# Values of two attention tiles as one group, and transposes moved between logits and scores, in an fp32 encoder layer

## The chip, the cores and the metric

The kernel runs on one core of one Trainium2 chip. The metric is the device time of one execution in microseconds. One more execution is recorded by the hardware profiler; the times of engines and instructions come from that one.

## The reference, cut to what matters

One encoder layer is applied to a prompt of 256 tokens and to a sample of 1024 tokens, all fp32, with a model width of 1024. After a normalisation and one wide projection, two attention branches run beside each other. Branch A has 8 heads of 64 with 2 key/value heads, a window of 128 to either side, a learned bias and a sink; branch B is a dilated mixture with 12 heads. Sigmoid gates merge both, then come an output projection and a squared-ReLU MLP. Branch A for one sequence is:

```python
s = einsum('bnqgrd,bnkgd->bngrqk', qb, kb) * (dh ** -0.5)
logits = where(valid, s + bias, NEG_INF)
m = maximum(max(logits, axis=-1), sink)
p = exp(logits - m[..., None])
denom = sum(p, axis=-1) + exp(sink - m)
o = einsum('bngrqk,bnkgd->bnqgrd', p, vb) / denom
...
merged = gates[:, :, 0] * (o_a @ w_branch_a) + gates[:, :, 1] * (o_b @ w_branch_b)
```

## The kernel before, in words

Tokens are cut into 10 tiles of 128 rows (8 of the sample, 2 of the prompt). The eight heads of branch A are four units of two heads. `order` lists the 40 pairs of unit and tile, and a loop takes two tiles per step: `for j in range(0, n + 2, 2)` with `n = 40`.

For one tile `scores` (lines 1063 to 1079) multiplies queries by the keys of the tile and its neighbours, two multiplications per head into one of two PSUM banks called `sc` (lines 1071, 1072). W is 384 keys, or 256 at the ends of a sequence. VectorE adds the bias and finds the row maximum in one instruction (line 1073), and writes the negated maximum (line 1077). `exponential` (line 1083) is one ScalarE instruction per head. `transposes` (line 1095) turns the probabilities block by block on TensorE: up to four blocks go into one bank `pt`, which ScalarE copies out (line 271), the remaining two into a second one, which VectorE copies out (line 273). There are two `pt` banks. `values_of` (line 1108) multiplies values by the turned probabilities. Its two heads fill the two halves of the partitions of one bank `pv`, of which there is one; the profile shows the form of these multiplications as 128\*64, where the others are 128\*128. VectorE copies the 128x128 result to a buffer `o` (line 1111, three buffers), and GpSimd's queue stores it to `scr_o[t]` (line 1112).

The same loop takes in other work, which its steps hand out piece by piece:

- `fill = logits()` multiplies the last gate columns of the wide projection. One `next(fill)` issues four 128x512 multiplications or eight 128x256 ones (line 192), three times per step. When a block of columns and tokens ends, the next `next(fill)` first issues ScalarE's copy of the result (line 1133) and its store, and after the 256-token block also `prepare()`: ScalarE rounds the next raw weights (line 231) and VectorE subtracts (line 235).
- `merges` combines the groups of branch B, four pieces per merge (lines 1165 to 1186), two pieces per step. The first piece also issues the loads of the next merge's rows on GpSimd's queue (lines 1146 to 1157) and ends in a small exponential on ScalarE (line 1169).
- `turn_merged` and `low_b` turn the merged rows of branch B in the last two full steps (lines 1214, 1222, 1226).

Each engine executes its own instructions in the order in which the program writes them here: `last.enter_context(tc.manual_schedule(engines=ALL))` fixes this until `last.close()`, after the loop and a short tail of it. What follows, the branch projections with `load_o` (line 1232), `turn_a` (lines 1250 to 1257), `low_a` (line 1261), the gates, and the rest of the layer, is ordered by a planner from its own estimates. `load_o(t)` loads the stored values of all units of a tile back, and `turn_a(t)` divides them by the sums of the exponentials, which `widen` (line 1240) spreads on GpSimd.

Of the kernel before, what the change touches and what calls it, by code (L numbers as in the profile page):

```python
# [15 lines left out]
P = 128  # L16
# [81 lines left out]
def encoder_kernel(  # L98
# [178 lines left out]
    scr_b = [dram.tile([T, 2, ROW], F32, name=f"scr_b{g}_") for g in range(3)]  # L277
    scr_o = [dram.tile([P, AH * HD], F32, name=f"scr_o{t}") for t in range(NT)]
    scr_x = [dram.tile([P, D], F32, name=f"scr_x{t}") for t in range(NT)]
# [769 lines left out]
    if True:  # L1049
# [13 lines left out]
        def scores(u, t):  # L1063
            st, bias = units[u]
            lo, W, c0 = tiles[t]
            s = a3("s", n=4)
            m = small.tile([P, 2], F32, name="m", tag="m")
# [31 lines left out]
        def values_of(u, t):  # L1099
            lo, W, _ = tiles[t]  # L1100
            pt = live.pop((u, t))
            v, rest = units[u][0]["v"]
            pv = bank("pv")
            for b in range(W // P):
                k = lo + b
                src = v[:, k, HALVES[u // 2]] if k < 8 else rest[:, k - 8, HALVES[u // 2]]
                for h in range(2):
                    nc.tensor.matmul(pv[HALVES[h], :P], src, pt[:, 2 * b + h, :],  # L1108
                                     start=b == 0, stop=b == W // P - 1, skip_group_check=True)
            o = a3("o", (P, P), 3)  # L1110
            nc.vector.tensor_copy(o, pv[:, :P])
            nc.gpsimd.dma_start(scr_o[t][:, P * u : P * u + P], o)

# [87 lines left out]
    if True:  # L1201
# [28 lines left out]
        def load_o(t):  # L1230
            rows_o[t] = slot("o", (P, 4, P))
            nc.sync.dma_start(rows_o[t], scr_o[t].rearrange("p (u q) -> p u q", u=4))

# [8 lines left out]
        def turn_a(t):  # L1242
            if t in (0, 4, 8):
                o_hi.block(t // 4)
                o_lo.block(t // 4)
            o = rows_o.pop(t)
            ps = bank("pt")
# [24 lines left out]
        for j in range(0, n + 2, 2):  # L1272
            if j < n:
                scores(*order[j])
                next(fill)
                if j > 2:
                    next(merges, None)
                next(fill)
                for h in range(2):
                    exponential(*order[j], h)  # L1280
                scores(*order[j + 1])
                next(fill)
                if j >= n - 4:
                    turn_merged(j - n + 4, "mm")
            if j:
                transposes(*order[j - 2])
            if j < n:
                exponential(*order[j + 1], 0)
            if j > 2:
                values_of(*order[j - 3])  # L1290
            if j:
                transposes(*order[j - 1])
            if j < n:
                exponential(*order[j + 1], 1)
            if j >= n - 4 and j < n:
                low_b(j - n + 4)
                turn_merged(j - n + 5, "mm")
            if j:
                values_of(*order[j - 2])
                if j > 2:  # L1300
                    next(merges, None)
            if j >= n - 4 and j < n:
                low_b(j - n + 5)
            if j < n and order[j][1] == 0 and order[j][0] < 3:
                u = order[j][0] + 1
                units[u] = load_unit(u), load_bias(u, lambda name, shape: a3(name, shape, 2))
            if j in (n - 6, n - 4):
                fetch()
            if j == n - 2:
                load_o(0)  # L1310
                load_o(1)
        next(fill)
        prepare()
        next(fill)
        values_of(*order[n - 1])
        run(merges)
# [570 lines left out]
```

## Time and profile before

| what | us |
|---|---|
| median of 3 runs (1727.32 to 1727.78) | 1727.51 |
| the profiled execution's own time | 1728.73 |
| its span, first to last instruction | 1727.0 |
| TensorE busy (matmuls, 98% of the span) | 1696.0 |
| TensorE weight loads busy (83%) | 1432.4 |
| VectorE / ScalarE / GpSimd busy | 978.5 / 727.4 / 525.7 |
| the loop of branch A, from about 562 to 712 | 150 |

PE stands for TensorE's matmuls and PEld for its weight loads, which overlap the matmuls; DVE is VectorE, ACT is ScalarE, POOL is GpSimd and SP the queue that issues most DMAs. A row of the timeline gives the start, the duration, the engine, the line, the operation, what is written and read with the shape, how many such instructions were put together, and in brackets the idle time of the engine ahead of it with what ended it. A row of the groups gives count, busy time, the mean duration in ns, and the idle time ahead of the group by what ended it. In a table of stretches there follow, after the bounds and the length, the busy times of PE, PEld, DVE, ACT and POOL, the granted clock, and the share and rate of DMA.

### The profile page before, as it was taken

The numbers are of one execution on the slowest core, as the hardware profiler recorded it, in microseconds if no ns is written. First come the engines' busy times: TensorE is split into PE (matmuls) and PEld (weight loads), VectorE is DVE, ScalarE is ACT, GpSimd is POOL, SyncE is SP. The second block draws the span as 40 slices with busy tenths as digits, with TensorE's granted clock in tenths as the row PEclk, the third lists the DMA queues.
The fourth block names the chain that finished last, engine by engine and source line by source line (L and its number), as shares of the span: only waits on it lengthen the run. The fifth ranks groups of instructions, "written<-read, shape, count | busy, mean of one in ns | idle before, by whom it ended". The sixth has DMA issues, their size and how long they took to land.

```text
span 1727.0 us, 25208 instructions
## 1 busy us (share of the span) xinstructions
PE 1696.0 (98%) x9248; PEld 1432.4 (83%) x9248; DVE 978.5 (57%) x1708; ACT 727.4 (42%) x1528; POOL 525.7 (30%) x462
## 2 busy tenths in 40 slices
PE   7999999999999999999999999999999999999998
PEld 6898888888888888788888788888888888888886
DVE  6733323445553577677458554545456786667575
ACT  6232223355553555655166433333334333333344
POOL 0212222212222354300100455555565442304050
PEclk9999999999999999999999999999999999999999
DMA  6414343576566753556012344334436834633333
GB/s 238 145 43 139 116 136 95 150 196 179 168 173 177 218 165 102 187 200 241 25 73 74 109 133 156 130 118 142 156 124 243 301 130 163 209 117 116 116 116 122
DMA packets 214779, 256.35 MB, mean 148 GB/s; under 512 B 24887, under 2 KB 144523, under 8 KB 214528
## 3 DMA queue, kind: packets, MB, share of 16 engines
q1 hardware_dynamic: 201424, 228.26, 41.0%
q0 software_dynamic: 12144, 24.38, 4.6%
q10 hardware_dynamic: 1088, 2.10, 0.3%
q8 instruction: 73, 1.20, 0.3%
q14 instruction: 50, 0.41, 0.1%
HBM read 169.10 MB, written 90.73 MB: 150 GB/s over the span
## 4 chain that ended last, share of the span: by engine, by line
PE 85%; DVE 4%; issue 3%; ACT 2%; DMA 2%; POOL 2%; SPq 0%; ACTq 0%; POOLq 0%; DVEq 0%
PE dn L351 21%; PE x L351 18%; PE mm L192 11%; PE z L351 9%; PE v L739 6%; PE pv L351 5%; PE mm L351 5%; PE y L351 4%; PE pv L566 2%; PE sc L522 1%; PE pt L553 1%; PE tr L342 1%; PE pv L1108 1%; PE pt L1095 1%; DVE clo L318 1%
## 5 line engine op out<-in xcount | busy, mean ns | idle before, releaser
L351 PE MATMUL dn<-dhi,ulo 128*128 128x512 f32 x448 | 174.7, 390 | 3.0 <-DVE ulo L186 3.0
L351 PE MATMUL dn<-dhi,uhi 128*128 128x512 f32 x448 | 174.3, 389 | 0.0
L351 PE MATMUL dn<-dlo,uhi 128*128 128x512 f32 x448 | 174.3, 389 | 0.0
L351 PE MATMUL x<-chi,wlo 128*128 128x512 f32 x424 | 167.6, 395 | 2.1 <-DVE u L1760 1.4
L351 PE MATMUL x<-clo,whi 128*128 128x512 f32 x424 | 165.7, 391 | 0.1
L351 PE MATMUL x<-chi,whi 128*128 128x512 f32 x424 | 165.1, 389 | 0.0
L318 DVE TENSOR_TENSOR wlo<-ta,whi 128x1024 fp32r<-128x1024 f32 x30 | 55.8, 1858 | 180.4 <-ACT whi L316 180.4
L318 DVE TENSOR_TENSOR wlo<-raw,whi 128x1024 fp32r<-128x1024 f32 x60 | 93.7, 1561 | 101.8 <-ACT whi L316 101.8
L393 POOL TENSOR_TENSOR tb<-raw 128x512 f32<-128x512 f32 x25 | 32.6, 1303 | 335.8 <-PE mm L192 113.5
L351 PEld LDWEIGHTS dn<-dhi,ulo 128*128 128x128 f32 x448 | 84.1, 188 | 21.7 <-DVE ulo L186 4.2
L186 DVE TENSOR_TENSOR ulo<-uraw,uhi 128x1024 fp32r<-128x1024 f32 x56 | 93.1, 1682 | 11.7 <-ACT uhi L185 11.7
L351 PEld LDWEIGHTS dn<-dhi,uhi 128*128 128x128 f32 x448 | 84.1, 188 | 17.6
L351 PEld LDWEIGHTS dn<-dlo,uhi 128*128 128x128 f32 x448 | 84.1, 188 | 17.2
L351 PEld LDWEIGHTS x<-chi,wlo 128*128 128x128 f32 x424 | 79.7, 188 | 20.3 <-issue 3.1
L351 PEld LDWEIGHTS x<-chi,whi 128*128 128x128 f32 x424 | 79.6, 188 | 17.1
L351 PEld LDWEIGHTS x<-clo,whi 128*128 128x128 f32 x424 | 79.8, 188 | 14.8 <-DVE clo L318 0.4
L1585 POOL TENSOR_TENSOR t<-raw,t 128x1024 f32<-128x1024 f32 x16 | 47.1, 2958 | 142.0 <-DMA raw<-in_w_down_dram 142.0
L1736 DVE TENSOR_TENSOR v<-v,dn 128x512 f32<-128x512 f32 x90 | 59.6, 683 | 42.8 <-PE dn L351 37.7
L1832 POOL TENSOR_TENSOR u<-u,u 128x640 f32<-128x640 f32 x16 | 25.6, 1597 | 165.1 <-ACT u L1757 165.1
L351 PE MATMUL pv<-phi,wlo 128*128 128x256 f32 x256 | 72.5, 283 | 1.7 <-ACT u L1756 1.7
L351 PE MATMUL dn<-dhi,up 128*128 128x512 f32 x224 | 73.5, 389 | 0.0
L543 ACT ACTIVATE s<-s,o 128x128 f32<-128x128 f32 (+1 forms) x120 | 51.9, 434 | 50.6 <-DVE o L535 46.6
(338 smaller groups left out, 4737.4 us busy)
## 6 DMA issues: line engine op xcount, KB each, us to landing
scr_u<-u SPq DMA_DIRECT2D x112, 320.0 KB, 2.6
uraw<-scr_u SPq DMA_DIRECT2D x56, 512.0 KB, 4.3
raw<-in_w_in_dram SPq DMA_DIRECT2D x33, 512.0 KB, 5.9
raw<-in_w_up_dram SPq DMA_DIRECT2D x32, 512.0 KB, 5.3
raw<-in_w_down_dram SPq DMA_DIRECT2D x28, 512.0 KB, 6.7
sg<-scr_g SPq DMA_DIRECT2D x32, 256.0 KB, 4.9
uraw<-scr_u SPq DMA_DIRECT2D x28, 256.0 KB, 4.4
v<-scr_v SPq DMA_DIRECT2D x96, 64.0 KB, 2.4
```

The lines of the kernel that those rows point to most:

```text
L186: nc.vector.tensor_tensor(lo, src, hi.bitcast(F32), op=ALU.subtract)
L192: nc.tensor.matmul(ps, a, b, start=i == 0, stop=i == len(seq) - 1)
L318: nc.vector.tensor_tensor(lo, src, hi.bitcast(F32), op=ALU.subtract)
L342: nc.tensor.transpose(ps[:, P * i : P * (i + 1)], xn[t][:, P * k : P * (k + 1)], ident)
L351: nc.tensor.matmul(ps, a, b, start=first and i == 0, stop=last and i == len(seq) - 1, skip_group_check=True)
L393: (nc.vector if vector else nc.gpsimd).tensor_tensor(o, x, y, op=ALU.subtract)
L543: nc.scalar.activation(s[:, h, :W], s[:, h, :W], AF.Exp, bias=nm[:, h : h + 1], accum_out=l[:, h : h + 1])
L566: nc.tensor.matmul(pv[p0 : p0 + nq, HD * h : HD * h + HD], pt[:, 2 * k + h, p0 : p0 + nq], v[:, a + k, HALVES[h]], start=k == 0, stop=k == ...
L739: nc.tensor.matmul(ps[:, :n], a, b, start=k == 0 and j == 0, stop=k == KC - 1 and j == 2)
L1585: nc.gpsimd.tensor_tensor(o, a, b, op=ALU.subtract)
L1736: nc.vector.tensor_tensor(v, v, ps, op=ALU.add)
L1832: nc.gpsimd.tensor_tensor(u[S1], u21, u22, op=ALU.add)
```

## The change

Four things change.

- `values_of(u, t)` now handles tiles t and t + 1. Their results stand beside each other in one `pv` bank, and one VectorE copy of 128x256 and one store move both. `o` has two buffers of 128x2x128.
- A step's values come one step later, all together between the step's first and second piece of `fill`. The transposes of the earlier step's first tile stand behind that second piece and ahead of the second tile's `scores`, and those of its second tile behind the third piece, at the step's end.
- The exponentials of the step's second tile stand behind both transposes. The first merge piece stands behind the values. The score buffer `s` has three buffers in place of four.
- `scr_o` holds pairs of tiles. `load_o` loads a pair at once, and `turn_a` takes its half.

```diff
-    scr_o = [dram.tile([P, AH * HD], F32, name=f"scr_o{t}") for t in range(NT)]
+    scr_o = [dram.tile([P, 4, 2, P], F32, name=f"scr_o{t}") for t in range(0, NT, 2)]
...
-            s = a3("s", n=4)
+            s = a3("s", n=3)
...
         def values_of(u, t):
-            lo, W, _ = tiles[t]
-            pt = live.pop((u, t))
-            v, rest = units[u][0]["v"]
+
             pv = bank("pv")
-            for b in range(W // P):
-                k = lo + b
-                src = v[:, k, HALVES[u // 2]] if k < 8 else rest[:, k - 8, HALVES[u // 2]]
-                for h in range(2):
-                    nc.tensor.matmul(pv[HALVES[h], :P], src, pt[:, 2 * b + h, :],
-                                     start=b == 0, stop=b == W // P - 1, skip_group_check=True)
-            o = a3("o", (P, P), 3)
-            nc.vector.tensor_copy(o, pv[:, :P])
-            nc.gpsimd.dma_start(scr_o[t][:, P * u : P * u + P], o)
+            for i in range(2):
+                lo, W, _ = tiles[t + i]
+                pt = live.pop((u, t + i))
+                v, rest = units[u][0]["v"]
+                for b in range(W // P):
+                    k = lo + b
+                    src = v[:, k, HALVES[u // 2]] if k < 8 else rest[:, k - 8, HALVES[u // 2]]
+                    for h in range(2):
+                        nc.tensor.matmul(pv[HALVES[h], P * i : P * i + P], src, pt[:, 2 * b + h, :],
+                                         start=b == 0, stop=b == W // P - 1, skip_group_check=True)
+            o = a3("o", (P, 2, P), 2)
+            nc.vector.tensor_copy(o, pv[:, : 2 * P].rearrange("p (i q) -> p i q", i=2))
+            nc.gpsimd.dma_start(scr_o[t // 2][:, u], o)
...
         def load_o(t):
-            rows_o[t] = slot("o", (P, 4, P))
-            nc.sync.dma_start(rows_o[t], scr_o[t].rearrange("p (u q) -> p u q", u=4))
+            if t % 2 == 0:
+                rows_o[t] = slot("o", (P, 4, 2, P))
+                nc.sync.dma_start(rows_o[t], scr_o[t // 2])
...
-            o = rows_o.pop(t)
+            o = rows_o[t - t % 2][:, :, t % 2, :]
...
             if j < n:
                 scores(*order[j])
                 next(fill)
-                if j > 2:
-                    next(merges, None)
-                next(fill)
                 for h in range(2):
                     exponential(*order[j], h)
+            if j > 2:
+                values_of(*order[j - 4])
+                if j < n:
+                    next(merges, None)
+            next(fill)
+            if j:
+                transposes(*order[j - 2])
+            if j == n:
+                next(fill)
+            if j < n:
                 scores(*order[j + 1])
                 next(fill)
                 if j >= n - 4:
                     turn_merged(j - n + 4, "mm")
             if j:
-                transposes(*order[j - 2])
+                transposes(*order[j - 1])
+                if j > 2:
+                    next(merges, None)
             if j < n:
-                exponential(*order[j + 1], 0)
-            if j > 2:
-                values_of(*order[j - 3])
-            if j:
-                transposes(*order[j - 1])
-            if j < n:
-                exponential(*order[j + 1], 1)
+                for h in range(2):
+                    exponential(*order[j + 1], h)
             if j >= n - 4 and j < n:
                 low_b(j - n + 4)
                 turn_merged(j - n + 5, "mm")
-            if j:
-                values_of(*order[j - 2])
-                if j > 2:
-                    next(merges, None)
-            if j >= n - 4 and j < n:
                 low_b(j - n + 5)
...
-        next(fill)
         prepare()
-        next(fill)
-        values_of(*order[n - 1])
+        values_of(*order[n - 2])
```

## The prediction

> **What bounds the kernel now.** I read the page's busy row first, then the busy time by stretches, then, for the one stage that the change touches (562 to 712 us), the weight loads in order of time and the table of waits.
>
> ```profile
> PE 1696.0 (98%) x9248; PEld 1432.4 (83%) x9248; DVE 978.5 (57%) x1708; ACT 727.4 (42%) x1528; POOL 525.7 (30%) x462
> 562.00:712.00 150.00, 147.85 (x1121) 123.08 (x1120) 97.80 (x394) 86.11 (x239) 67.00 (x110) 1.00 0.54 159
> 622.18 0.63 PEld L1108 LDWEIGHTS pv<-pt,va 128*64 128x64 f32 x12 [0.17 <-PE pt L1095]
> 622.98 0.64 PEld L1095 LDWEIGHTS pt<-ident,s 128*128 128x128 f32 x6 [0.17 <-issue]
> 623.79 0.63 PEld L1108 LDWEIGHTS pv<-pt,va 128*64 128x64 f32 x12 [0.17 <-issue]
> 624.59 0.19 PEld L1071 LDWEIGHTS sc<-kp,qp 128*128 128x128 f32 x1 [0.17 <-issue]
> ```
>
> The second line reads, after the length: PE 147.85, PEld 123.08, DVE 97.80, ACT 86.11, POOL 67.00 us, then a clock of 1.00. TensorE is the bound, and the vector engines have a third of the stage free. The four lines below are one step's tail: values (V, L1108), transposes (T, L1095), values, then the next logits (S, L1071). V runs in the form 128\*64, everything else in 128\*128. At each change of form the loads stop for 0.17 us, although nothing is late. That this is the form, and not the operation, is seen where transposes are followed by plain multiplications in one form:
>
> ```profile
> 721.12 0.59 PEld L1250 LDWEIGHTS pt<-ident,wl 128*128 128x128 f32 x4
> 721.68 0.19 PEld L192 LDWEIGHTS mm<-obhi,wlo 128*128 128x128 f32 x1
> ```
>
> 721.12 + 0.59 is 721.71, and the next load starts at 721.68: no gap.
>
> Is there anything to gain, when PE is busy 147.85 of 150 us? By the busy row at most 2.15 us. The starts say more: six transposes take 0.64 us of loads, but V follows them after 0.81 (622.98 to 623.79). A matmul's recorded duration overlaps the next one's, so it covers the gap. The Trainium skill ("Trainium Kernel Development and Optimization", Performance Expectations) calls matmul busy time a bad metric for this reason and weight-load busy a good one; by its rule the room here is read from PEld, and the gaps above bear that out. I go by starts and gaps. The busy row stays as a rival.
>
> **The change, part by part.** *Changes of form.* Now a step is S, fill, fill, S, fill, T, V, T, V (a fill is four 128x512 multiplications, L192, or eight 128x256). Then it is S, fill, V V, fill, T, S, fill, T. The V groups of both tiles become one, and only its two ends change form. Count for before: 2 changes in the second step, 4 in each of 19 steps, 2 around the last V: 80. After: 20 groups, 40. The waits of the stage bear the 80 out:
>
> ```profile
> PEld pv L1108 <- issue: 4.4, 21, 0.9
> PEld pt L1095 <- issue: 3.1, 18, 0.2
> PEld sc L1071 <- issue: 2.9, 17, 0.2
> PEld pv L1108 <- PE pt L1095: 2.0, 12, 0.2
> PEld pt L1095 <- ACT pt L271: 1.4, 3, 0.6
> PEld pt L1095 <- DVE pt L273: 1.3, 2, 0.7
> PEld pv L1108 <- DVE o L1111: 0.8, 5, 0.2
> ```
>
> (total us, times, longest): 21 + 12 + 5 into V, 18 + 3 + 2 into T, 17 into S, and a few single ones. Saved: 40 x 0.17 = 6.8 us.
>
> The trace has no V right behind a fill. The nearest row has another narrow form behind a 128x512 multiplication:
>
> ```profile
> 358.24 0.39 PE L351 MATMUL x<-chi,whi 128*128 128x512 f32 x1
> 358.56 0.71 PE L522 MATMUL sc<-qk 64*128 64x128 f32 x8
> 705.17 0.50 PE L192 MATMUL mm<-hhi,whi 128*128 128x512 f32 x1
> 705.51 0.39 PE L192 MATMUL mm<-hhi,wlo 128*128 128x512 f32 x1
> 705.74 0.40 PE L192 MATMUL mm<-hlo,whi 128*128 128x512 f32 x1
> ```
>
> There the start comes 0.32 us after the last multiplication's, against 0.23 from one to the next (705.51 to 705.74): 0.09 extra. The last three rows stand right behind a V: the first interval is 0.34, 0.11 more than 0.23, since the first weights cannot be loaded ahead. So entering V from a fill costs between 0.09 and 0.28 (0.17 + 0.11); I take the 0.17 of the edges that have rows. The first-weights cost behind V falls once per step before (on S) and once after (on the fill), and cancels. T in front of S has no row; the row of T in front of L192 says 0, and at most it is again 0.11, twice in each of 20 steps, 4.4 us. I take 0. With these ends the term lies between a gain of 6.8 - 20 x 0.11 - 4.4 = 0.2 and of 6.8 + 20 x 0.08 = 8.4 us; taken, 6.8.
>
> *Copies and stores.* Two 128x128 copies of V and two stores per step become one of 128x256 and one. DVE falls from 2 x 0.291 to about 0.424, POOL from 2 x 0.557 to one; neither is on the path in the loop. The store now waits for V's copy in mid-step, and the merge's row loads queue behind it on POOL; they are issued two steps, 14 us, ahead of their use, and POOL is idle 78.1 us ahead of its stores, so I price that at nothing too. The loads of o halve in number (10 to 5 on SP, 0.37 us of issue each); that saves SP under 2 us beside PE and is priced at nothing: the weights' fetch and gate loads queued behind them only come earlier.
>
> ```profile
> L1111 DVE COPY o<-pv 128x128 f32<-128x128 f32 x40 | 11.6, 291 | 21.6 <-PE pv L1108 18.2 <-DMA scr_o<-o 2.9
> L1112 POOL DMA_DIRECT2D scr_o<-o x40 | 22.2, 557 | 78.1 <-DVE o L1111 52.5 <-PE sc L1072 14.0 <-DVE z L1173 8.7
> L273 DVE COPY pt<-pt 128x256 f32<-128x256 f32 x24 | 10.2, 424 | 13.7 <-PE pt L1095 13.7
> L1232 SPq DMA_DIRECT2D o<-scr_o x10: 319/367/393, 698.2 to 734.0; - x10
> 707.79 0.45 PEld L1108 LDWEIGHTS pv<-pt,vp 128*64 128x64 f32 x8 [0.94 <-issue]
> 707.38 0.29 DVE L1111 COPY o<-pv 128x128 f32<-128x128 f32 x1 [2.94 <-DMA scr_o<-o]
> ```
>
> The last two rows are the loop's end. Four stores in a row run out of three o buffers, DVE waits 2.94 us for one to land, and the last V waits 0.94 for its single bank, 0.77 beyond the usual gap. With one store per 7 us and two buffers this wait goes. In its place V of the last two tiles now follows the last transposes directly: the second tile needs ACT's copy (0.60) of four transposes just issued, while the first tile's eight multiplications cover 0.43; I put 0.4 for it (0 to 0.7).
>
> *Waits that the new order moves.* Beyond the usual gap TensorE now loses in the loop:
>
> ```profile
> 573.44 0.20 PEld L1095 LDWEIGHTS pt<-ident,s 128*128 128x128 f32 x2 [0.49 <-ACT pt L271]
> 580.43 0.42 PEld L1095 LDWEIGHTS pt<-ident,s 128*128 128x128 f32 x4 [0.33 <-ACT pt L271]
> 581.50 0.20 PEld L1095 LDWEIGHTS pt<-ident,s 128*128 128x128 f32 x2 [0.65 <-DVE pt L273]
> 650.81 0.42 PEld L1095 LDWEIGHTS pt<-ident,s 128*128 128x128 f32 x4 [0.58 <-ACT pt L271]
> 651.88 0.20 PEld L1095 LDWEIGHTS pt<-ident,s 128*128 128x128 f32 x2 [0.66 <-DVE pt L273]
> ```
>
> The first is two T in a row sharing two banks; the new order parts them, and 0.5 goes. The others (0.8 and 1.1) lie in two of the four steps in which a fill also splits weights (L231 on ACT, then L235 on DVE). In the new order that split stands between V and T, so the copies of T queue behind it and T of the next tile needs their banks. Worked through for the worst such step, from its S at 0, with these durations:
>
> ```profile
> L1083 ACT ACTIVATE s<-s,nm_a 128x384 f32<-128x384 f32 x48 | 29.1, 607 | 7.8 <-DVE nm_a L1077 7.6
> L1073 DVE CUSTOM_DVE_ANT_0 s<-sc,bias 128x384 f32<-128x384 f32 x48 | 24.7, 553 | 4.7 <-PE sc L1072 3.2 <-ACT e L1169 1.1 <-ACT s L1083 0.4
> L231 ACT ACTIVATE whi<-raw 128x1024 fp32r<-128x1024 f32 x5 | 5.3, 1055 | 0.2 <-issue 0.2
> L235 DVE TENSOR_TENSOR wlo<-raw,whi 128x1024 fp32r<-128x1024 f32 x5 | 6.1, 1225 | 4.6 <-ACT whi L231 4.6
> L271 ACT ACTIVATE pt<-pt 128x512 f32<-128x512 f32 x40 | 23.8, 595 | 16.5 <-PE pt L1095 15.9 <-ACT obhi L1222 0.2
> ```
>
> PE: S to 0.7, fill to 1.6, V (0.17 + 1.28) to 3.1, gap and fill to 4.2, T to 4.8, S to 5.5, fill to 6.4, then the next T, first bank at 6.4, second at 6.9. ACT ends both exponentials near 4.2, then the merge's small one and the gate's store copy by 5.1, L231 by 6.2, the copy of T (0.60) by 6.8. DVE: L235 to 7.4, its copy of T to 7.8, two logit reductions to 8.9. T is 0.4 late on ACT and 0.6 more on DVE; the next S, wanting its second bank at 8.5, waits 0.5 for the reductions: 1.5 us. Without the merge's exponential in that step it is 0.7, and I put the first, where the raw weights land late, at 1.2. Four steps: 1.2 + 0.7 + 1.5 + 0.7 = 4.1 against 1.9 now, +2.2 (0 to +5). The exponentials of a step's second tile (2 x 0.61) move behind both copies of T on ACT and so into the next step's start; their own transposes come a whole step later, so only the first tile's exponentials queue behind them, done by 4.2 as above. The remaining 16 steps: the second S now stands 2.3 us before the next S where it stood 4.8 before. In between, DVE has the copy of T and two reductions, 0.42 + 2 x 0.55 = 1.5 us; 0.8 is spare, so I price it at nothing, and this is the cover that a rival takes away.
>
> *The end.* Behind the stage one wait hangs on the same late chain:
>
> ```profile
> 719.87 0.19 PEld L192 LDWEIGHTS mm<-obhi,wlo 128*128 128x128 f32 x1 [0.80 <-ACT gs L1133]
> ```
>
> DVE's 2.94 us fall away ahead of it; I take 0.3 of the 0.8 (0 to 0.8).
>
> **Sum.** -6.8 (form) -0.8 (pv bank) +0.4 (last V) -0.5 (first T) +2.2 (splits) -0.3 (end) = -5.8 us. The profiled execution took 1728.73 us (span 1727.0), so 1722.9; the median of the runs, 1727.51, lies 1.2 lower and gives 1721.7, the prediction.
>
> **The rivals.** *DVE becomes the bound of a step (slower).* If the copies of T start over 0.8 us late in ordinary steps too, because the wide copy of V (0.42) and a merge piece (up to 1.0) now stand ahead of them, then each next S waits for its reduction. It decides from a delay of 0.8 + 0.35 (what a step gains): at 1.4 us late a step loses 0.6, 16 steps 9.6, and the time is 1721.7 + 9.6 = 1731.3. For it: DVE is busy 97.80 of 150 us and the new wait has less slack. Against: by the sequence above DVE is idle from about 4.8 until T ends.
>
> *The gain is given back (no change).* Split steps at their upper price (+2.8 more), or the planner, which orders everything behind the stage by its own estimates, placing pieces worse. In 712 to 745 PE is idle 33.00 - 30.81 = 2.2 us, so doubling that costs as much:
>
> ```profile
> 712.00:745.00 33.00, 30.81 (x153) 24.75 (x152) 23.67 (x48) 23.34 (x47) 7.04 (x10) 1.00 0.75 264
> ```
>
> One of the two leaves 1723.9 to 1724.5, both 1726.7.
>
> *The busy row is right.* Then at most 2.15 us are there: 1725.4, no change. Against it stand the starts.
>
> **How the numbers follow.** Forecast 0.68, own range 1717.9 to 1724.0 (below: the form term 1.6 better and the splits free, 1721.7 - 1.6 - 2.2; above: splits dearer by 2.3). DVE bound 0.12; given back 0.15; busy row 0.05. About 0.2% (3.5 us) is what a measurement of this kernel can tell from no change, so faster is below 1724.0: 0.68 and 0.02 of the second rival's lower end, 0.70; same 0.17, the rest of the second rival (0.13, less 0.01 that ends slower) and the third (0.05); slower 0.12 and that 0.01, 0.13. The range runs to 1727.5 above, leaving the slower rival out, and to 1717.5 below: the forecast's own end less 0.5, all of the 0.8 at the end instead of 0.3.
>
> **What would show it.** Right: in the changed profile 24 loads of L1108 in a row with one gap on either side, L1095 without a gap in front of L1071, about 40 gaps of 0.17 in place of 80, PEld still about 123 us busy in a stage about 6 us shorter, no wait of L1111 on its store. Split steps wrong: waits of L1095 on L271 and L273 other than about 4 us in total. The DVE rival: waits of L1071 on L1073 in most steps. The sum is wrong if entering V behind a fill shows over 0.28 us, or if a gap appears between T and S.

## The result, and the profile after

The changed kernel takes 1722.92 us (median of 9 runs, 1722.12 to 1724.1); the kernel before, in the 9 runs beside them, 1727.91 (1727.32 to 1732.47). The ratio is 0.9967, interval 0.9957 to 0.9977: 5.0 us faster. Forecast were 1721.7 and a gain of 5.8. The profiled execution took 1723.0 us, with a span of 1721.2.

First the busy row and the same two stretches as before, then the waits of the weight loads in 562 to 712 us (total us, times, longest):

```profile
PE 1690.8 (98%) x9248; PEld 1430.4 (83%) x9248; DVE 973.6 (57%) x1688; ACT 727.0 (42%) x1528; POOL 516.2 (30%) x442
562.00:712.00 150.00, 147.61 (x1140) 124.55 (x1139) 98.05 (x381) 89.50 (x243) 57.22 (x91) 1.00 0.53 156
712.00:745.00 33.00, 31.78 (x156) 25.52 (x155) 23.79 (x49) 22.55 (x50) 6.79 (x10) 1.00 0.85 303
...
PEld pv L1110 <- issue: 4.1, 12, 0.4
PEld mm L192 <- issue: 3.4, 20, 0.2
PEld pt L1095 <- DVE pt L273: 1.9, 4, 0.7
PEld pt L1095 <- ACT pt L271: 1.8, 2, 0.9
PEld sc L1071 <- DVE m L1073: 1.8, 8, 0.3
PEld pv L1110 <- ACT s L1083: 1.1, 3, 0.4
PEld pv L1110 <- ACT pt L271: 0.4, 1, 0.4
PEld pv L1110 <- ACT obhi L1224: 0.2, 1, 0.2
```

PE is busy 147.61 of 150 us, as good as before (147.85), although the stage has become shorter: the matmul row could not show this gain. In the waits, 20 gaps in front of L192 (the fill behind the values) and 16 in front of L1110 take the place of the 80; four more in front of L1110, behind a fill of 128x256, are 0.13 long and too short to be listed. (The one 0.4 on L271 lies inside the last group and is no change of form.) The rows "pt <- issue", 18 times before, and "sc <- issue", 17 times, are gone. New are the eight waits of L1071 on L1073.

One ordinary step in order of time, first its weight loads, then the multiplications around the values:

```profile
616.44 0.19 PEld L192 LDWEIGHTS mm<-hhi,whi 128*128 128x128 f32 x1
616.99 1.29 PEld L1110 LDWEIGHTS pv<-pt,va 128*64 128x64 f32 x24 [0.36 <-issue]
618.45 0.19 PEld L192 LDWEIGHTS mm<-hhi,wlo 128*128 128x128 f32 x1 [0.17 <-issue]
...
619.26 0.81 PEld L1095 LDWEIGHTS pt<-ident,s 128*128 128x128 f32 x6
620.03 0.19 PEld L1071 LDWEIGHTS sc<-kk,q 128*128 128x128 f32 x1
...
616.44 0.40 PE L192 MATMUL mm<-hlo,whi 128*128 128x512 f32 x1
616.67 0.39 PE L192 MATMUL mm<-hhi,whi 128*128 128x512 f32 x1
616.99 1.53 PE L1110 MATMUL pv<-pt,va 128*64 128x128 f32 x24
618.45 0.50 PE L192 MATMUL mm<-hhi,wlo 128*128 128x512 f32 x1
618.79 0.40 PE L192 MATMUL mm<-hlo,whi 128*128 128x512 f32 x1
```

24 value loads stand in a row, with one gap on either side. What they cost is read from the multiplications: the first V starts 0.32 after the last fill, against 0.23 from fill to fill (616.44 to 616.67): 0.09, and within 0.01 the same at all 18 groups that stand behind a fill. The loads' gap of 0.36 is thus mostly time in which the fill still multiplies. The way back shows its 0.17, and the first fill's interval is 0.34, so 0.11 more: 0.37 per group. Between T and S there is no gap: 619.26 + 0.81 is 620.07, and the next load starts at 620.03. That bears out the term that had no row before and was taken as nothing.

### The profile page after: what moved, and what is told of

Its sections match the earlier page's. It is cut to its first block, busy times and chain, and to the rows that moved or that the text cites. A ratio compares the mean times of both kernels' runs of the same rounds, so it can differ in the third digit from the quotient of the medians.

```text
span 1721.2 us, 25157 instructions
## 1 busy us (share of the span) xinstructions
PE 1690.8 (98%) x9248; PEld 1430.4 (83%) x9248; DVE 973.6 (57%) x1688; ACT 727.0 (42%) x1528; POOL 516.2 (30%) x442
## 4 chain that ended last, share of the span: by engine, by line
PE 87%; DVE 4%; ACT 2%; issue 2%; DMA 2%; POOL 1%; SPq 0%; DVEq 0%; ACTq 0%; POOLq 0%
PE dn L351 21%; PE x L351 18%; PE mm L192 12%; PE z L351 9%; PE v L739 5%; PE pv L351 5%; PE mm L351 5%; PE y L351 4%; PE pv L566 2%; PE sc L522 2%; PE pt L553 1%; PE pv L1110 1%; PE pt L1095 1%; PE tr L342 1%; DVE clo L318 1%
## 5 line engine op out<-in xcount | busy, mean ns | idle before, releaser
L318 DVE TENSOR_TENSOR wlo<-raw,whi 128x1024 fp32r<-128x1024 f32 x60 | 89.4, 1491 | 102.2 <-ACT whi L316 102.2
L543 ACT ACTIVATE s<-s,o 128x128 f32<-128x128 f32 (+1 forms) x120 | 51.9, 434 | 50.5 <-DVE o L535 46.5
```

The lines of the kernel that those rows point to most:

```text
L318: nc.vector.tensor_tensor(lo, src, hi.bitcast(F32), op=ALU.subtract)
L543: nc.scalar.activation(s[:, h, :W], s[:, h, :W], AF.Exp, bias=nm[:, h : h + 1], accum_out=l[:, h : h + 1])
```

## The experiments

To compare the runs I split the loop, from the first S to the first turned weight of the output projection, into three parts. *Waits* are the weight loads' idle times beyond 0.17 us at a change of form (0.36 where V follows a fill), and all over 0.14 elsewhere, the one in front of that turned weight included. *Half clock* is the time lost while the granted clock was 0.5 (told with the seventh kernel below). The *rest* is the loop without both; all in us, from the profiled executions.

| kernel | changes of form | loop | waits | half clock | rest |
|---|---|---|---|---|---|
| before | 80 | 154.7 | 3.1 | 0 | 151.6 |
| before, again | 80 | 157.0 | 4.0 | 1.7 | 151.3 |
| before, split late, fetch early | 80 | 160.1 | 8.9 | 0 | 151.2 |
| values apart | 78 | 158.7 | 6.9 | 0 | 151.8 |
| **changed** | 40 | 151.3 | 5.9 | 0 | 145.4 |
| split late | 40 | 148.5 | 3.3 | 0 | 145.2 |
| fetch early | 40 | 149.6 | 3.8 | 0 | 145.7 |
| three mendings | 40 | 148.1 | 2.9 | 0 | 145.2 |
| old place | 40 | 154.3 | 8.0 | 1.7 | 144.6 |
| stores per tile | 40 | 153.6 | 6.7 | 1.7 | 145.3 |
| old place, calm | 40 | 163.2 | 15.3 | 5.1 | 142.8 |
| four tiles | 20 | 160.7 | 15.3 | 5.1 | 140.3 |
| four, late | 20 | 156.0 | 11.2 | 3.4 | 141.4 |
| four, calm | 20 | 150.2 | 6.7 | 1.7 | 141.8 |

Apart from two rows, the rest goes by the count of changes alone: 151.2 to 151.8 with about 80, 144.6 to 145.7 with 40, 141.4 and 141.8 with 20. That is 0.15 us for one change between the first two and 0.19 between the last two. What differs between kernels of one count are waits. Count and place are crossed here: the old place with 40 changes has 144.6, the new order with 78 has 151.8. (The old place, calm, and the four tiles lie 2 and 1 us below their groups. They are the two with three spells of half clock and over 15 us of waits; the split probably counts something twice there, and what that is was not found.)

**1. The group in its old place.** Two tiles' values as one group, but the other parts in the old order, V V between the step's two transposes. For room, `pt` has three buffers and `o` one.

```diff
-            pt = a3("pt", (P, 6, P), 2)
+            pt = a3("pt", (P, 6, P), 3)
-            o = a3("o", (P, 2, P), 2)
+            o = a3("o", (P, 2, P), 1)
...   # order of a step: S, fill, fill, S, fill, T, V V, T
```

> The order of before, but the values of both tiles form one group a step later, between the two transposes at the step's end (T VV T); one copy and one store per pair; three pt buffers, one o buffer. No piece of the fill moves. If the changes of form carry the gain: two per step as in the changed kernel, about 0.32 us per step against 0.71, so 19 x 0.39 = 7.4 us off the loop, and the weight splits stay where they were: 1720 to 1722 us. If the gain came from moving the transposes between logits and scores, or from waits that the new place took away: 1726 to 1728, like before.

Measured: 1727.33 (1725.56 to 1730.56), ratio 0.9992 (0.9983 to 1.0001): no gain is left, and the time is the rival's. Yet the rest, 144.6, says that the changes of form fell as meant; waits (8.0) and half clock (1.7) took it back. VectorE's own waits, in the same 150 us, show where they come from:

```profile
DVE s L1073 <- PE pt L1095: 27.3, 15, 3.2
...
DVE o L1113 <- DMA scr_o<-o: 6.1, 3, 2.9
```

In the old order four score tiles are alive at the second S of a step, two being made and two not yet turned. With three `s` buffers the reductions (L1073) wait for transposes, 15 times; no such row stands in either kernel's waits. And the copy of V waits for its only buffer's store. So this run does not price the place by itself; it shows that three score buffers are too few in the old order, while in the new one, with T before the second S, nothing waits for them.

**2. The values apart again.** The order of the changed kernel, but the second tile's V behind the first tile's transposes; `pt` has three buffers and `o` one.

```diff
-                values_of(*order[j - 4])
+                values_of(*order[j - 4], (0,))
...   # fill, transposes of the first tile
+            if j > 2:
+                values_of(*order[j - 4], (1,))
```

> The changed kernel, but the second tile's values stand behind the first transposes, so a step is S, fill, V, fill, T, V, S, fill, T: four changes of form again, everything else as changed (one copy, one store, pair layout; three pt buffers, one o buffer). If the forms carry the gain: 19 x 0.33 = 6.3 us slower than the changed kernel, about 1729 us. If place or waits carry it: 1723, as changed.

Measured: 1734.17 (1731.49 to 1738.96), ratio 1.0033 (1.0019 to 1.0048): 11 us slower than the changed kernel where 6 were expected. The rest is back at 151.8 (78 changes), +6.4, as the theory wants. Of what is left in the profiled execution, waits are 0.9 more, 0.5 is a later first S, and 1.7 lie behind the loop, between first and last turned weight; that execution is itself 1.8 below the median, and what the others lose more is not known. VectorE waited 13.0 us in all for its stores; the row of waits from 560 to 720 us:

```profile
DVE o L1117 <- DMA scr_o<-o: 13.0, 4, 3.6
```

**3. The split late.** The changed kernel with the weight split at its step's end, behind the exponentials.

```diff
-                        prepare()
+                        due.append(1)
...   # at the end of the step
+            if due:
+                due.pop()
+                prepare()
```

> The changed kernel, but the weights' split (L231 and L235) that a fill's piece set off is written at the step's end, behind the second tile's exponentials. The changed profile shows 2.1 + 0.8 + 0.9 + 0.8 = 4.6 us of waits in the four split steps. If they come from the split standing between V and T: 2.5 to 4 us go, 1719 to 1720.5 us. If the split only displaces its wait (the next reductions then queue behind it): 1722 to 1723.5.

Measured: 1721.59 (1720.35 to 1723.02), ratio 0.9956 (0.9943 to 0.9969). The loop's waits fall from 5.9 to 3.3, the lower end of what was expected, the median by 1.3, less than was expected. Of the 2.6 us, 0.9 is the wait at 607 us, which does not stand in a split step (the merge's rows, below); in the four split steps the waits fall from 4.6 to 2.9. So the place between V and T costs 1.8 us of waits; the other 2.9 stay, 1.7 of them now behind the exponentials, as the rival had it in part. The 0.4 at the last values is as in the changed kernel.

**4. Copies and stores by tile.** The changed kernel, but with two 128x128 copies of V, two stores, three `o` buffers of a tile, and loads by tile.

```diff
-            o = a3("o", (P, 2, P), 2)
-            nc.vector.tensor_copy(o, pv[:, : 2 * P].rearrange("p (i q) -> p i q", i=2))
-            nc.gpsimd.dma_start(scr_o[t // 2][:, u], o)
+            for i in range(2):
+                o = a3("o", (P, P), 3)
+                nc.vector.tensor_copy(o, pv[:, P * i : P * i + P])
+                nc.gpsimd.dma_start(scr_o[t + i][:, P * u : P * u + P], o)
```

> The changed kernel with a copy, a store and a load of o for each tile again (three o buffers of 128x128, ten loads at the end), the group and the order as changed. By the prediction these are off the path: 1723, same within 0.5. If the halved loads and stores carry the 1.2 us that the stretch behind the loop gained, about 1724.1, and up to 1724.5 if DVE again waits for a store at the loop's end.

Measured: 1725.09 (1723.71 to 1727.16), ratio 0.9979 (0.9971 to 0.9988): 2.2 slower than the changed kernel, where no difference was expected. A store and a later copy, what waits for them, and then the stores between 595 and 612 us and those of the whole profile (count, KB, median us to landing):

```profile
597.71 0.58 POOL L1115 DMA_DIRECT2D scr_o<-o  x1 [0.38 <-DVE o L1114]
...
607.35 0.29 DVE L1114 COPY o<-pv 128x128 f32<-128x128 f32 x1 [3.60 <-DMA scr_o<-o]
...
608.16 0.21 ACT L1172 ACTIVATE e<-e 128x12 f32<-128x12 f32 x1 [4.27 <-DVE e L1171]
...
609.61 0.20 PEld L1095 LDWEIGHTS pt<-ident,s 128*128 128x128 f32 x2 [2.77 <-ACT pt L271]
...
scr_o<-o POOLq DMA_DIRECT2D x4, 64.0 KB, 8.3
...
scr_o<-o POOLq DMA_DIRECT2D x40, 64.0 KB, 2.0
```

Where a unit's keys, values and biases are loaded, a store takes 8.3 us, over the whole profile 2.0. That is no trait of this variant: in the same stretch the median is 7.2 in the kernel before and 6.3 in the changed one. But three tiles' buffers last one and a half steps and run out here; two pairs last two steps. VectorE stands 3.60 us, ScalarE waits for the merge's work behind it, the transposes wait 2.8 for ScalarE's copy, and the clock halves. So the layout by pairs, priced at nothing, is worth about 2 us by the medians, and the trace shows buffer depth as the place; copies, stores and loads were not tried one by one.

**5. Four tiles in a group.** Values of four tiles every second step, `pt` with four buffers, `o` with one, and fewer narrow buffers elsewhere (`N_Q` 5 for 8).

```diff
-                values_of(*order[j - 4])
+                if j % 4 == 2:
+                    moving = values_of(order[j - 6], order[j - 4])
+                    next(moving)
...   # after the second tile's transposes: run(moving) copies and stores the second pair
```

> The changed kernel, with the values of four tiles as one group in every second step, one bank for the four, four buffers of the transposed probabilities, one buffer of the copied values, and the second pair's copy and store at the step's end. Ten entries into values and ten ways back fall away. Theory forms: a group costs about 0.38 us (0.09 to 0.13 at the first values, 0.18 back to a fill, 0.11 in the first fill's interval), so 10 x 0.38 = 3.8 us less than the changed kernel, about 1718 to 1720, with 20 gaps of form in the loop where the changed kernel has 40. Rival, absolute times: TensorE only arrives earlier at copies and loads that land when they did, and gets back half or less: 1721 to 1723. Rival, longer wait of the copies: a group of twice the length puts off the next transposes and so the copies of ScalarE and VectorE, and the step without values leaves those engines short: waits of over 5 us more than now, 1724 to 1727.

Measured: 1734.64 (1733.42 to 1736.12), ratio 1.0035 (1.0021 to 1.0049). It is slower than every range given. The rest falls by 5.1, against 3.8 by the theory of forms; this is one of the two rows that the split puts too low, and the two other kernels of four tiles fall by 4.0 and 3.6. Waits of 15.3 bury it, 1.3 of them in front of the first turned weight. VectorE and the weight loads in order of time:

```profile
610.79 0.42 DVE L1116 COPY o<-pv 128x256 f32<-128x256 f32 x1 [5.66 <-DMA scr_o<-o]
...
611.93 0.55 DVE L1073 CUSTOM_DVE_ANT_0 s<-sc,bias 128x384 f32<-128x384 f32 x1
...
612.54 0.19 PEld L1071 LDWEIGHTS sc<-kk,q 128*128 128x128 f32 x1 [4.15 <-DVE m L1073]
```

The copy waits for the only buffer's store, the reduction stands behind the copy, and the next S behind the reduction.

**6. Four tiles, split late.** The same, with the split at its step's end and a fill ahead of the last V.

> As the kernel with four tiles in one group, and the weight split written at the end of its step, behind the exponentials, and one fill put ahead of the last values. Theory forms: the gain of the late split in pairs (about 1.3 us) comes on top of the groups' 3.8, so about 5 us below the changed kernel, 1717 to 1719; the last values' wait of 0.40 goes as well. Rival: in the steps without values the copies of the transposes are what TensorE waits for whether a split stands there or not; then the same time as the kernel with four tiles alone, within 1 us.

Measured: 1732.59 (1729.89 to 1734.47), ratio 1.0023 (1.0013 to 1.0033). 2 us better than without, as neither theory nor rival had it; the waits on the one buffer stay (one S waits 4.76).

**7. The kernel before, once more.** One execution, for two things: the 1.65 us that lie ahead of the loop between the two profiles, and how steady the loop before is.

> The kernel before once more, unchanged. In the shown profile of it the first score of branch A's loop starts at 563.75 us, 1.65 later than in the changed kernel, though the code ahead of the loop is the same. Theory: that is the run and not the change; here the first score starts between 562.1 and 563.2, as in the runs of the variants, and the stretch from the first score to the first turned weight is again 154.7 (154 to 155.5). Rival: the change moves something ahead of the loop (the addresses of its buffers, say); then 563.7 comes again.

Measured: 1730.26 in the profiled execution. The first S starts at 563.06. So it moves by 0.7 from one execution of the same kernel to another; over all kernels here it lies between 562.0 and 563.8. The traces say where the 1.65 arises: 0.95 at the start of the program, where the 128x512 multiplications (L739) follow each other in 0.43 us up to 16.0 us in both executions of before, in the changed kernel only up to 13.9, and in 0.23 from there; and 0.7 in one wait for an exponential (L543) at 472 us, which neither of the other two has. Variants of the changed kernel lie 0.1 below it to 1.1 above. So I hold the 1.65 to be no part of the change. The loop is 157.0, not the 154 to 155.5 that was expected. Three rows of the timeline, and a stretch's row, where the granted clock, 0.53, stands behind the five busy times:

```profile
579.26 1.23 DVE L235 TENSOR_TENSOR wlo<-raw,whi 128x1024 fp32r<-128x1024 f32 x1 [2.86 <-ACT whi L231]
580.95 0.42 PEld L1095 LDWEIGHTS pt<-ident,s 128*128 128x128 f32 x4 [1.54 <-ACT pt L271]
582.02 0.20 PEld L1095 LDWEIGHTS pt<-ident,s 128*128 128x128 f32 x2 [0.65 <-DVE pt L273]
...
582.70:586.10 3.40, 3.40 (x19) 2.85 (x14) 2.60 (x13) 0.93 (x4) 0.91 (x2) 0.53 0.14 47
```

In the split step whose raw weights land late, the old order too waits, by a varying amount: 0.33 in the first profile, 1.54 here. And here the clock was halved for 3.4 us behind it, which is the 1.7 of the table's column.

**8. The second fetch early.** The changed kernel with the raw weights' second fetch ahead of the loop's loads.

```diff
+        fetch()
         load_h21()
...
-                    if i + 1 < len(PLAIN) and t0 == 0:
+                    if 0 < i and i + 1 < len(PLAIN) and t0 == 0:
                         fetch()
```

> The changed kernel, with only the second fetch of raw weights issued ahead of the loads in front of the loop, not inside the first unit's preparation. Theory: in the fifth step ScalarE's half of the split waits 0.85 us for the raw weights' DMA, and everything behind it on ScalarE and VectorE comes as much later; TensorE's waits of 2.1 us in that step become like the other three split steps' (0.8 to 0.9), so 1.2 to 1.5 us less than the changed kernel: 1721.4 to 1721.7. Rival: the waits come from the split's own length, and the DMA only hides in it: within 0.4 us of the changed kernel. Rival: the earlier fetch delays the loads ahead of the loop and the loop begins later: no gain or up to 1 us more.

Measured: 1722.89 (1722.5 to 1723.22), ratio 0.9968 (0.9955 to 0.998): the changed kernel's time. The mechanism is right and the time is not: waits in the step j = 4 (the third; the expectation calls it the fifth) fall from 2.1 to 0.9, the 0.9 in the step at 607 us go as well, and the loop is 1.8 shorter. Of that, 0.55 is the later first S, which stands in the trace from 15 us on, far ahead of the moved fetch, and 0.9 is lost between first and last turned weight, where a wait stands that the changed kernel lacks (712 to 762 us):

```profile
PEld mm L192 <- ACT sg L1341: 1.0, 1, 1.0
```

Whether the moved fetch causes it was not tried by itself; the ninth kernel moves the fetch too and has no such wait.

**9. Three mendings.** Late split, early fetch, and one of the fills behind the last V ahead of them.

```diff
         prepare()
+        next(fill)
         values_of(*order[n - 2])
...   # and the late split and the early fetch as above
```

> The changed kernel with three places mended: the split at the end of its step, the second raw fetch ahead of the loop, and one of the fills behind the last values moved ahead of them. Theory: of the 5.9 us of waits of the loop the split steps' 4.6 fall to about 1.5 and the last values' 0.40 goes, so 3.0 to 3.5 us below the changed kernel, about 1719.5 (1718.5 to 1720.5), and 1 to 2 below the kernel with the late split alone. Rival: the late split alone has got all there is, the rest being bound by the copies behind the transposes: the same as that kernel within 0.5 us, about 1721.5.

Measured: 1720.2 (1720.07 to 1721.06), ratio 0.9954 (0.9941 to 0.9966); the fetch-early kernel on the same chip had no run below 1722.5. This is the fastest of all by its median, 1.4 below the late split alone, but those were measured on different chips, and the two profiled executions took 1720.2 and 1720.35. The loop has 2.9 us of waits against 3.3 there, less by the 0.4 at the last values alone; so with the late split in place the early fetch shows nothing in the loop. In the table of waits from 560 to 720 us, none of L1071 is left, and L1095 has these:

```profile
PEld pt L1095 <- ACT s L1083: 1.7, 2, 0.9
PEld pt L1095 <- ACT pt L271: 0.7, 2, 0.4
PEld pt L1095 <- issue: 0.4, 1, 0.4
```

The exponentials, behind the late split now, are what the transposes wait for.

**10. The kernel before with the mendings.** Late split and early fetch in the old order.

> The kernel before, with the two mendings that the changed kernel got in an earlier run: the weight split at its step's end and the second raw fetch ahead of the loop. Its loop has 3.1 us of waits beyond the gaps of form, against 5.9 in the changed kernel. Theory: the gaps of form stay (80 of them), only the waits at the splits go, 1 to 1.5 us: 1726 to 1727, so that with splits mended on both sides the change is worth 6 to 7 us and not 5. Rival: the mendings are worth as much here as there (2.7 us): about 1725, and the splits had nothing to do with the change.

Measured: 1733.49 (1731.75 to 1734.23), ratio 1.0031 (1.0019 to 1.0043): 5.5 us slower than the kernel before, against both expectations. The split's end stands right ahead of the next step's first S in both orders. In the old one VectorE has the merge's work there too, and S finds its banks taken (timeline of one such step, then the waits of 562 to 712 us):

```profile
582.60 1.23 DVE L235 TENSOR_TENSOR wlo<-raw,whi 128x1024 fp32r<-128x1024 f32 x1 [1.52 <-ACT whi L231]
...
584.84 0.55 DVE L1073 CUSTOM_DVE_ANT_0 s<-sc,bias 128x384 f32<-128x384 f32 x1
...
585.45 0.19 PEld L1071 LDWEIGHTS sc<-kk,q 128*128 128x128 f32 x1 [1.77 <-DVE m L1073]
...
PEld sc L1071 <- DVE m L1073: 7.6, 8, 1.8
```

So the late split is no mending by itself; where it pays depends on the order around it.

**11. The old place, calm.** As the first, with two `o` buffers, late split, early fetch, `N_Q` 7.

> One group of values for two tiles, but in the old place, behind the step's last transposes, as in the first variant; here with two buffers of the copied values (the first variant had one, and its copies waited 6.1 us on stores), the split at the step's end, the second fetch ahead of the loop, and one narrow buffer fewer elsewhere to make room. 40 gaps of form. Theory: forms carry the gain wherever the group stands, and what ate it in the first variant were the late buffer and the splits: 1720 to 1722. Rival: the old place itself costs, since TensorE comes to transposes, scores and values earlier than the exponentials and copies are done: 1724 to 1727.

Measured: 1735.57 (1733.91 to 1742.78), ratio 1.0054 (1.004 to 1.0069), slower than both ranges. (The group stands between the two transposes, as in the first kernel.) The three score buffers remained, and the late split came on top, which the tenth kernel shows to be harmful in this order. VectorE's waits in 562 to 712 us:

```profile
DVE s L1073 <- PE pt L1095: 35.1, 18, 3.2
```

What a group in the old place would give with four score buffers was not tried.

**12. Four tiles, calm.** As the sixth, with two `o` buffers, the early fetch, `N_Q` 4.

> Four tiles' values as one group, as before with the split at the step's end and a fill ahead of the last values, but with two buffers of the copied values (with one, the copies waited 10 to 12 us on stores, up to 6.3 at once, and scores waited 4.2 and 4.8 behind them), the second fetch ahead of the loop, and one narrow buffer fewer. 20 gaps of form. Theory: the single buffer was what lost it; without those waits the loop is 3 to 4 us shorter than the paired kernel with the same mendings (1720.2): 1716 to 1718. Rival: the groups of four lose by their length, since copies and exponentials come in bursts, and waits of several us stay: 1722 to 1728. Second rival: fewer narrow buffers delay loads, which would show as waits of the logits or splits on DMAs.

Measured: 1724.32 (1723.18 to 1727.02), ratio 0.9979 (0.9971 to 0.9988). In the rival's range, not the theory's, and 8.3 us better than the sixth. VectorE's waits on stores, 10.2 us there, are gone, and with them the S wait of 4.76; half clock takes 1.7 in place of 3.4. The fetch and `N_Q` changed too, so the buffer's share is not shown by itself. The loop, 150.2, is now below the changed kernel's, though 2.2 above the paired one with the same mendings, with waits of 6.7 (a 2.2 in the first step, 1.4 twice). It then loses 2.5 behind the loop, from last turned weight to the end (964.2 against 961.7 us in the ninth kernel). That the missing narrow buffers cause this is likely: from last turned weight to the end it is 960.8 to 961.7 us in all kernels with 7 or 8 of them, 962.7 and 962.3 with 5, and 964.2 with 4. But no run restores them alone. Both rivals hold in part.

## Why the prediction was right, point by point

- **The room is in the loads' gaps, not in the busy row.** Right. The busy row allowed 2.15 us at most; the rest fell by 6.2, with PE as busy as before. The Trainium skill ("TensorEngine Tiling (Array Packing)", Key Properties) says that a change of the tiling mode, not only of the tile, drains TensorE; the counts 80, 40 and 20 in the table agree, and give it 0.15 to 0.19 us here.
- **Changes of form, -6.8.** Measured -6.2 (151.6 to 145.4). T in front of S costs nothing, as taken. Entering V from a fill cost 0.09, the lower of the two bounds and not the 0.17 taken, which alone would be 1.6 us better over 20 groups. That the sum is smaller all the same means that the old changes cost less than their gap in the loads: 6.2 and 20 groups at 0.37 are 13.6 us, less 20 x 0.11 for first weights 11.4, over 80 changes 0.14 each. So the term came out near because two errors ran against each other.
- **The last V, -0.8 and +0.4.** Right in mechanism, the first a little large. The V that waited 0.94 before stands right behind a fill (so there was one such V in the trace, though a late one); beyond the 0.36 of that place its wait was 0.6, not 0.8. L1113 waits on no store any more, and the predicted wait on ScalarE's copy stands at its place with its size:

```profile
L1113 DVE COPY o<-pv 128x256 f32<-128x256 f32 x20 | 8.5, 424 | 13.7 <-PE pv L1110 13.1 <-DMA r<-scr_b__82 0.6
...
701.96 0.42 PEld L1110 LDWEIGHTS pv<-pt,vp 128*64 128x64 f32 x8 [0.17 <-issue]
702.77 0.42 PEld L1110 LDWEIGHTS pv<-pt,vp 128*64 128x64 f32 x8 [0.40 <-ACT pt L271]
```

- **The first T, -0.5.** Right; the wait is gone.
- **The splits, 4.1 against 1.9.** Right in mechanism and near in size: 2.1, 0.8, 0.9 and 0.8, in sum 4.6. By step I had 1.2, 0.7, 1.5 and 0.7: the first was put too low, the third too high. The first is the one with the late raw weights:

```profile
577.00 1.06 ACT L231 ACTIVATE whi<-raw 128x1024 fp32r<-128x1024 f32 x1 [0.85 <-DMA raw<-in_w_in_dram]
577.97 0.58 ACT L271 ACTIVATE pt<-pt 128x512 f32<-128x512 f32 x1
578.10 1.23 DVE L235 TENSOR_TENSOR wlo<-raw,whi 128x1024 fp32r<-128x1024 f32 x1 [2.47 <-ACT whi L231]
578.60 0.42 PEld L1095 LDWEIGHTS pt<-ident,s 128*128 128x128 f32 x4 [0.94 <-ACT pt L271]
...
579.71 0.20 PEld L1095 LDWEIGHTS pt<-ident,s 128*128 128x128 f32 x2 [0.69 <-DVE pt L273]
580.18 0.19 PEld L1071 LDWEIGHTS sc<-kk,q 128*128 128x128 f32 x1 [0.27 <-DVE m L1073]
```

  ScalarE waits 0.85 for the raw weights, then splits, then copies T; VectorE's half comes behind it, and T and S stand in line for both. The chain is the predicted one.
- **The merge's row loads behind the store, priced at nothing.** Wrong, by 0.9. The store now waits for V's copy, and the row loads stand behind it on GpSimd's queue. In one step they land too late; VectorE's merge work waits for them, ScalarE's small exponential for that, and ScalarE's copies of T stand behind the exponential:

```profile
605.05 0.16 DVE L1167 TENSOR_TENSOR mm__6123<-r 128x4 f32<-128x4 f32 x1 [1.64 <-DMA r<-scr_b__82]
...
605.81 0.21 ACT L1171 ACTIVATE e<-e 128x12 f32<-128x12 f32 x1 [2.38 <-DVE e L1170]
...
606.62 1.08 ACT L271 ACTIVATE pt<-pt 128x512 f32<-128x512 f32 x2
607.26 0.20 PEld L1095 LDWEIGHTS pt<-ident,s 128*128 128x128 f32 x2 [0.89 <-ACT pt L271]
```

  The lead was not the 14 us that I counted. The eight loads are issued one after another from 591.71 to 595.93 us, and VectorE is free for them at 603.4: 7.5 us after the last issue, which lands after 9.3. In the kernel before it was 10.1 us and a landing after 6.9. So 2.6 us of lead went, and the landing took 2.4 longer. That transfers on this queue are slow where a unit is loaded could have been read from the profile before: its stores took 7.2 us there (595 to 612 us) against 2.5 in all. Why the landing was slower still in the changed kernel is open, and so is the part of the store ahead of the rows: no run takes it away, and the wait was gone both with the fetch moved early and with the split moved late, where the last rows still land a little late (VectorE waits 0.5 and 0.7 for them).
- **Copies and stores by pairs, priced at nothing.** The prediction looked only at engine time. The fourth kernel is about 2 us slower without them, and its trace shows late stores and one buffer too few. It did not spoil the sum, because before had the same three tiles' buffers and, with the stores spread over the step, ran out only at the end.
- **DVE as the bound of a step (the slower rival).** Did not come: L1071 waits for L1073 in the split steps alone, 1.8 us in all.
- **The end, -0.3.** From first to last turned weight it is 1.2 less (47.55 to 46.34); the 0.80 wait is gone whole. This stretch was between 46.1 and 48.0 over all kernels, and three runs of the old order had 47.55 each, so part of it seems to belong to the change, but not to a part that I could name: with loads by tile (fourth kernel) it is 47.4, but also 47.2 to 48.0 in four kernels with loads by pair.
- **The sum.** (By its own terms the range's lower end is 1717.4, not 1717.5.) In the loop I forecast -5.5 (all terms but the end) and the two first profiles show -3.4: the splits 0.5 more, the merge rows 0.9, the form term 0.6 and the last V 0.2 smaller. Behind the loop I forecast -0.3, and there and ahead of it they show -2.3, of which the 1.65 ahead is, by the seventh kernel, no part of the change. That the total of these two executions came near, 5.7 us against 5.8, is luck to that extent. Against the second profile of before the loop's gain is 5.7, so the size of the miss hangs on which execution of before is taken.

## What to carry to other kernels

Count changes of the multiplications' form as instructions with a price of their own (0.15 to 0.19 us here) and read it from the gaps of the weight loads, since matmul busy time hides it. Regrouping gains that price only as long as no buffer is one too few: the variants here that saved changes and lost a buffer of `s` or `o` gave back most or all of it. A load or a split that is moved must be placed by what stands next on ScalarE and VectorE in that order; the late split gained about 1.3 us in one order, and with the early fetch it lost 5.5 in the other.

## What the hardware showed that was not expected

The granted clock fell to 0.5 for spells of 3.4 us in the middle of the loop, at a loss of 1.7 us each, half of the spell. Some stood behind long TensorE waits (4.1 with four tiles; 4.8 with four, late, where the spell was 6.8 us), but others behind short ones: 1.54 and 0.65 close together (the kernel before, again), 2.4 to 2.5 (old place, calm, three times), 2.2 (four tiles, calm), 2.8 (stores per tile). Not every such wait did it: the kernel before with the split late had four waits of 1.7 to 1.8 and the old place, calm, one more of 2.5 without it. The Trainium skill ("TensorE: Matmul & The Clock Gate", Part 1: The HAM clock gate) has the clock halved after at least one idle window of about 3.4 us, with windows that run freely. The 3.4 us of half clock and the dependence on more than a wait's length agree with that; the waits do not, since most of them were shorter than a whole window. So a wait of 1.54 us with one of 0.65 behind it was followed by a loss of 1.7 more. A variant's time is less steady for it: the slowest execution of the old place, calm, 1742.78 us, has a mean granted clock of 0.992, its fastest, 1733.91, 0.997.

Stores from GpSimd's queue took far longer to land where units are loaded (595 to 612 us) than in the whole profile, by the median: 7.2 against 2.5 us in the kernel before, 6.3 against 2.2 in the changed one, 8.3 against 2.0 with stores per tile.
